# A two-layer hybrid encoder on one core: small operations moved between VectorE, ScalarE and GpSimd, maxima taken two key tiles later, one post step per key tile

## The chip, the cores and the metric

The kernel runs on 1 core of one Trainium2 chip. The metric is the device time of one execution in microseconds. The engines are called as in the profile: PE is TensorE (PEld its weight loads), DVE is VectorE, ACT is ScalarE, POOL is GpSimd, SP is SyncE, which issues nearly all DMAs.

## The reference

Two layers work on x of 2048 tokens by 1024 channels, in float32. What one layer computes, shortened:

```python
h = rmsnorm(x, pre_g[l])
u_a, v_a, g_a, q, k, v, g_b = split(h @ w_in[l])       # 512 512 512 512 128 128 512
y_a = gmlp_group(u_a, v_a, ...) * silu(g_a)            # layernorm of v_a, a 128x128 matrix
                                                       # per group over chunks of 128 tokens
y_b = gqa_axial_attention(q, k, v, ...) * silu(g_b)    # 8 query heads, 2 kv heads, head_dim 64
out = concat(y_a, y_b) @ w_out[l]
x = x + rmsnorm(out, post_g[l])
```

Queries and keys are normed per head and rotated (2-D axial rotary) before a full softmax attention over all 2048 keys.

## The kernel before

**Precision.** A float32 operand is split into a rounded "hi" and a residual "lo" (hi by ScalarE, lo by a subtraction on VectorE or GpSimd), and each product is the sum of hi·hi, hi·lo and lo·hi, the three `PASSES`.

**Projection stage (`Project.run`).** The 2048 tokens are four groups of 512, worked on in two halves of two groups. For a group, `hT_jobs` loads token tiles of 128 rows, norms them (two squares on ScalarE, a chain of small VectorE instructions `rsqrt_row_steps`, a multiplication by the gain row `g_row`), transposes them on TensorE and splits them into hi and lo. Blocks of 256 columns of w_in are loaded and split (`load_w`, `split_w`), and TensorE multiplies: keys and values (`do_kv`), queries (`do_q`), v_a (`do_va`), the attention gate (`do_gb`), the gMLP gate and u (`do_gate`). Small jobs are put off with `bg.add(delay, f)` and run by `bg.tick()`, which is called between the matmuls of a projection.

**g_row.** `norm_row` loads the norm gain, broadcast to 128 rows, and scales it by a constant (L185). For layer 0 it is called with the first token tile. For layer 1 it is asked for at key tile 1 of layer 0's attention, but as it is not pinned in order it is issued as soon as its buffer is free, which in the profile is inside layer 0's second projection half.

**Spatial weights.** `spatial_weights` transposes the gMLP matrices on TensorE into PSUM, copies them into `wsT` (L233), splits them and stores the parts to DRAM, from which they are loaded again as `ws`. Its four later jobs `b` compute a bias in PSUM and copy its two halves into `zbias` (L249, L250).

**Keys.** `k_t` holds hi and lo of the transposed keys. Rows 64 and 65 of the lo part hold ones (the memset at L1187), so that the second score matmul, whose query operand carries minus the maximum of each query row in two rows, subtracts that maximum while it adds the lo part.

**Attention stage (`attend`).** 32 units (4 query blocks of 512 by 8 heads) with 16 key tiles each make 512 key tiles in one loop over `k`. A key tile has two score matmuls into a bank `sp`, two exponentials by ScalarE (a float16 one, `p_hi`, and a float32 one, `p_f`), their difference `p_lo` (by GpSimd, for 15 of 100 key tiles by VectorE), and, some tiles later, the products with v and with ones (`po`, `sums`). Into this loop other work is woven:

- `later`, a table from key tile to jobs. For a later unit u, 16 steps `max_step` (a matmul into `pmax`, a VectorE maximum) are laid over `span` = 20 key tiles from `k0`; `max_row` follows at `k0 + span + 1`, `stack_max` at `k0 + span + 3`. The latter transposes the maxima on TensorE, makes two rows of them on ScalarE and VectorE, and stores them by two DMAs; `load_q` reads them back for the unit's scores.
- `fill`, a list of output steps: the product with w_out of an earlier query block, spread over the key tiles. A token tile's two halves are squared by ScalarE and multiplied by `g_post` on VectorE.
- `post_queue`: once a token tile's output is complete, `post_steps` appends the steps of its norm: eight small VectorE instructions, two residual adds of 128x512, the store, and, in layer 0 for the first eight token tiles, also layer 1's pre-norm (two squares, eight small steps, two scalings, a store to `h_d`), 24 steps in all. Up to two are taken in each key tile (L1107).

In the last query block the product with w_out is finished behind the attention (`last_steps`): there `post_steps` also multiplies by `g_post` in four pieces of 128x256 per token tile (`gain`, on GpSimd), and two token tiles' steps alternate.

**Order.** All instructions issued through `PE`, `ACT`, `DVE` and `POOL` keep their program order on their engine; this holds for all of the attention loop. Those through `nc.vector`, `nc.scalar`, `nc.gpsimd` and `nc.sync` are placed by a planner, which takes the earliest in program order among those that it holds to be ready, and may bring one far forward. Buffers come from rotating pools; token rows, `g_post`, `x_r` and `o_t` share five buffers "row", PSUM has seven banks "ps" beside `sums`.

Of the kernel before, what the change touches and what calls it, by code (L numbers as in the profile page):

```python
# [14 lines left out]
ALU = mybir.AluOpType  # L15
# [4 lines left out]
P = 128  # L20
# [5 lines left out]
HD = 64  # L26
# [8 lines left out]
NORM_SCALE = -8192.0 / D ** 0.5  # L35
# [3 lines left out]
def encoder(ctx: ExitStack, tc, x, w_in, w_out, pre_g, post_g, ln_a_g, ln_a_b,  # L39
# [135 lines left out]
    class Project:  # L175
# [5 lines left out]
        def norm_row(self):  # L181

            self.g_row = lay.tile([P, D], F32, name="g_row")
            nc.sync.dma_start(self.g_row, pre_g[self.l].partition_broadcast(P))
            nc.scalar.mul(self.g_row, self.g_row, 1.0 / NORM_SCALE)  # L185

        def begin(self):

# [26 lines left out]
        def spatial_weights(self):  # L215
            l = self.l
            self.lng = lay.tile([P, 4], F32, name="lng")
            nc.sync.dma_start(self.lng, ln_a_g[l].rearrange("(t p) -> p t", p=P))
            self.zbias = lay.tile([P, 4, P], F32, name="zbias")
            wsT = row_t("wsT")  # L220
            for hf in range(2):
                raw = f_t("fa")
                nc.sync.dma_start(raw.rearrange("p (g j) -> p g j", g=4),
                                  spatial_w[l, 4 * hf:4 * hf + 4].rearrange("g i j -> i g j"))
                hi = f_t("fh", dt=F32R)
                lo = f_t("fl", dt=F32R)

                def t(hf=hf, raw=raw, hi=hi, lo=lo):
                    ps = ps_t("pt")
                    for g in range(4):  # L230
                        PE.transpose(ps[:, g * P:(g + 1) * P], raw[:, g * P:(g + 1) * P], ident)
                    sl = slice(hf * GRP, (hf + 1) * GRP)
                    nc.vector.tensor_copy(wsT[:, sl], ps)  # L233
                    nc.scalar.copy(hi, wsT[:, sl])
                    nc.gpsimd.tensor_tensor(lo, wsT[:, sl], hi.bitcast(F32), ALU.subtract)
                    nc.sync.dma_start(ws_d[:, 0, sl], hi.bitcast(F32))
                    nc.sync.dma_start(ws_d[:, 1, sl], lo.bitcast(F32))
                bg.add(WS_DELAY + 2 * hf, t)
            lnb = f_t("fb")
            nc.sync.dma_start(lnb, ln_a_b[l].partition_broadcast(P))  # L240
            sb = row_t("sb_row", (1, D))
            nc.sync.dma_start(sb, spatial_b[l:l + 1].rearrange("o g i -> o (g i)"))
            for c in range(4):
                def b(c=c):
                    ps = ps_t("pt")
                    PE.matmul(ps[:, 0:2 * P], lnb[:, c * P:(c + 1) * P], wsT[:, 2 * c * P:(2 * c + 2) * P],
                              start=True, stop=False)
                    PE.matmul(ps[:, 0:2 * P], ones1, sb[:, 2 * c * P:(2 * c + 2) * P], start=False, stop=True)
                    nc.vector.tensor_copy(self.zbias[0:HD, c, :], ps[0:HD, 0:P])  # L249
                    nc.vector.tensor_copy(self.zbias[HD:P, c, :], ps[HD:P, P:2 * P])  # L250
                bg.add(WS_DELAY + 8 + 2 * c, b)

        def load_w(self, cols):
# [267 lines left out]
        def run(self, kv, first, last_jobs, first_wo):  # L521
# [5 lines left out]
            for n, gs in enumerate(halves):  # L527
                if len(gs) > 1:
                    hTs[gs[1]], preps, trans = self.hT_jobs(gs[1])
                    late = self.l == 0 and n == 0  # L530
                    for j, f in enumerate(preps):
                        if late:
                            bg.add(8 + j, f)
                        else:
                            f()
                    for m, f in enumerate(trans):
                        bg.add((13 if late else T_DELAY) + 3 * m // 2, f)
                if n == 0:
                    self.gains()
                w = self.split_w(self.load_w([C_Q]))  # L540
                for i, g in enumerate(gs):
                    if i == 0:
                        for f in self.stores:
                            f()
                        self.stores = []
                    if i == len(gs) - 1:
                        raw = self.load_w([C_Q + WB])
                    self.do_kv(g, self.banked(hTs[g], w_kv))
                    if i == len(gs) - 1:
                        w_next = self.split_w(raw)  # L550
                        raw = self.load_w([C_VA])
                    self.do_q(g, self.banked(hTs[g], w), 0)
                if n == 0:
                    self.spatial_weights()
                w = w_next
                for i, g in enumerate(gs):
                    self.do_q(g, self.banked(hTs[g], w), 1)
                    if i == 0:
                        w_next = self.split_w(raw)
                w = w_next  # L560
                raw = self.load_w([C_VA + WB])
                ws = [row_t("ws", dt=F32R) for _ in range(2)]
                for i in range(2):
                    nc.sync.dma_start(ws[i].bitcast(F32), ws_d[:, i])
                w = [w, self.split_w(raw)]
                raw = self.load_w([C_GB])
                for g in gs:
                    vs = []
                    for j in range(TPG):
                        ps = self.proj_tok(hTs[g], j, w[0])  # L570
                        self.proj_tok(hTs[g], j, w[1], ps, WB)
                        v = f_t("fv")
                        nc.scalar.copy(v, ps)
                        vs.append(v)
                    self.do_va(g, vs, ws)
                w = self.split_w(raw)
                blocks = [[C_GB + WB]] + [[C_GA + c * P, C_U + c * P] for c in range(4)]
                if n + 1 < len(halves):
                    blocks.append([C_K])
                if n + 1 == len(halves):  # L580
                    self.scale_v()
                    last_jobs()
                for b in range(2):
                    raw = self.load_w(blocks.pop(0))
                    for i, g in enumerate(gs):
                        self.do_gb(g, self.banked(hTs[g], w), b)
                        if i == 0:
                            w_next = self.split_w(raw)
                    w = w_next
                for c in range(4):  # L590
                    raw = self.load_w(blocks.pop(0)) if blocks else None
                    for i, g in enumerate(gs):
                        if i == len(gs) - 1 and c == 3 and n + 1 < len(halves):
                            g2 = halves[n + 1][0]
                            hTs[g2], preps, trans = self.hT_jobs(g2)
                            for j in range(TPG):
                                preps[j]()
                            for m, f in enumerate(trans):
                                bg.add(6 + 2 * m, f)
                        pg = self.proj_ch(hTs[g], w, 0)  # L600
                        pu = self.proj_ch(hTs[g], w, P)
                        self.do_gate(g, c, pg, pu)
                        if i == 0 and c == 3 and n + 1 == len(halves):
                            hTs[g] = None
                            first_wo()
                        if i == 0 and raw is not None:
                            w_next = self.split_w(raw)
                    w = w_next
                w_kv = w
                bg.flush()  # L610
# [18 lines left out]
    def attend(l, kv, nxt):  # L629
# [25 lines left out]
        def at(k, f):  # L655
            later.setdefault(k, []).append(f)
# [298 lines left out]
        def post_steps(s, t, last=False):  # L955
            z = small.tile([P, 1], F32, name="rs_o", bufs=4)

            def gain(i):
                sl = slice(i * WB, (i + 1) * WB)
                return lambda: POOL.tensor_tensor(s.o[:, sl], s.o[:, sl], g_post[:, sl], ALU.mult)  # L960

            def add(hf):
                def f():
# [80 lines left out]
        for u in range(pre, len(units)):  # L1044
# [3 lines left out]
            for n in range(steps):  # L1048
                at(k0 + n * span // steps, lambda u=u, n=n: max_step(u, n, PE, DVE))
            at(k0 + span + 1, lambda u=u: max_row(u, DVE))  # L1050
            at(k0 + span + 3, lambda u=u: stack_max(u, PE, ACT, DVE))

        def load_gb(u):
            qb, h = units[u]
# [37 lines left out]
        for k in range(end + 4):  # L1092
            if k < total:
# [10 lines left out]
                ACT.activation(p_f(k), sp, AF.Exp)  # L1104
                if not dve_share(k):
                    sub_lo(k, POOL)
            for _ in range(2):  # L1107
                if post_queue:
                    post_queue.pop(0)()
            kb = k - 1  # L1110
            if 0 <= kb < total and dve_share(kb):
                sub_lo(kb, DVE)
# [68 lines left out]
    for l in range(DEPTH):  # L1181
# [2 lines left out]
        v_t = big_t([P, 2, NT * NKV * HD], "v_st")  # L1184
        kv.append(v_t.bitcast(F32)[:, 0].rearrange("p (t k d) -> p t k d", t=NT, k=NKV))
        kv.append(v_t.bitcast(F16)[:, 1].rearrange("p (t k d) -> p t k d", t=NT, k=NKV))
        nc.vector.memset(kv[1][HD:HD + 2], 1.0)  # L1187
        att = attend(l, kv, layers[l + 1] if l + 1 < DEPTH else None)
        layers[l].run(kv, layers[l].first, *next(att))
        for _ in att:  # L1190
# [41 lines left out]
```

## Time and profile before

| | |
|---|---|
| time of three runs | 2773.86, 2774.44, 2772.46 us; median 2773.86 |
| the profiled execution's own time | 2771.47 us |
| its span (first to last instruction) | 2769.3 us |
| mean granted TensorE clock | 0.992 |
| busy: PE, DVE, ACT, POOL | 2677.1, 1896.8, 1522.7, 1287.0 us |

The times say how long an execution takes; the profile shows one execution. A timeline row gives start, duration, engine, line, operation, output<-input, shape and count, and in brackets how long the engine stood idle before it and what released it. A row of the waits gives who waited for whom, the total in us, how often, and the longest. A row by windows gives the window and its length, the busy time of PE, PEld, DVE, ACT and POOL with instruction counts, the granted clock, the DMA engines' share and GB/s. Line 84 is the helper through which every pinned instruction goes, so that these are told apart by the names of their tiles.

### The profile page before, as it was taken

Reading aid. Unit: us, or ns where it says so; the run is one execution under the profiler, and the core shown is the slowest. Engines: PE = TensorE matmul, PEld = TensorE weight load, DVE = VectorE, ACT = ScalarE, POOL = GpSimd, SP = SyncE. Lnnn points to the kernel's source line nnn. Section 1 sums busy time; section 2 is a strip of 40 time slices with the busy share of each in tenths; the row PEclk is TensorE's granted clock in tenths of the full one; section 3 lists DMA queues with packets and bytes.
Section 4 is the critical chain, followed back from the end, with each engine's and each line's share of the span. In section 5 each row is a group of like instructions: output and inputs, shape, how many; then the busy total and the mean of one; then the engine's idle time right before and its main releaser. Section 6 shows DMA issues by size and latency. Waiting matters only on the chain.

```text
span 2769.3 us, 48428 instructions
## 1 busy us (share of the span) xinstructions
PE 2677.1 (97%) x18230; PEld 1782.0 (64%) x18230; DVE 1896.8 (68%) x3796; ACT 1522.7 (55%) x3005; POOL 1287.0 (46%) x1080
## 2 busy tenths in 40 slices
PE   7999999999999999999999999999999999999997
PEld 6898899764444444444589989997644444444444
DVE  8862688876666776776487528888766666666664
ACT  4221432117887787787732214221288877778774
POOL 1210122007786676776632101210277767667765
PEclk9999999999999999999999999999999999999999
DMA  4424522322222232222354334333322222221313
GB/s 143 146 81 127 165 76 81 112 63 89 89 71 81 75 98 79 82 80 80 110 179 138 115 114 134 88 92 98 94 64 72 82 70 73 81 76 47 112 46 129
DMA packets 275310, 265.31 MB, mean 96 GB/s; under 512 B 19202, under 2 KB 233346, under 8 KB 275076
## 3 DMA queue, kind: packets, MB, share of 16 engines
q1 hardware_dynamic: 275076, 262.22, 30.2%
q8 instruction: 143, 2.34, 0.3%
q14 instruction: 91, 0.75, 0.1%
HBM read 177.09 MB, written 85.07 MB: 95 GB/s over the span
## 4 chain that ended last, share of the span: by engine, by line
PE 77%; DVE 11%; ACT 5%; DMA 3%; issue 2%; POOL 1%; SPq 0%; DVEq 0%; POOLq 0%; ACTq 0%
PE pp L84 27%; PE sp L84 14%; PE po L84 11%; PE pout L84 11%; PE pmax L84 7%; PE sums L84 4%; PE pt L84 2%; DVE fc L363 2%; ACT p_parts L84 2%; ACT p_f L84 2%; DMA w_raw<-in_w_in_dram 1%; DVE mx L84 1%; DVE o_t L84 1%; DVE w_lo L268 1%; ACT w_hi L267 1%
## 5 line engine op out<-in xcount | busy, mean ns | idle before, releaser
L84 POOL TENSOR_TENSOR p_parts<-p_f,p_parts 128x512 f16<-128x512 f32 x872 | 1034.9, 1205 | 404.2 <-ACT p_f L84 304.3
L84 ACT ACTIVATE p_parts<-sp 128x512 f16<-128x512 f32 x1024 | 630.0, 615 | 296.5 <-PE sp L84 289.8
L84 DVE TENSOR_REDUCE mx<-pmax 128x1 f32<-128x512 f32 x768 | 513.0, 681 | 211.9 <-PE pmax L84 209.9
L84 PE MATMUL pout<-wo,y_t 128*128 128x512 f32 x1488 | 657.1, 506 | 0.7 <-ACT p_f L84 0.3
L84 PE MATMUL po<-p_parts,v_st 128*32 128x512 f16 (+1 forms) x3072 | 639.2, 383 | 0.2
L84 ACT ACTIVATE p_f<-sp 128x512 f32<-128x512 f32 x1024 | 632.0, 617 | 0.0
L84 PE MATMUL pp<-w_hi,hT 128*128 128x256 f32 x3584 | 502.5, 290 | 16.1 <-DVE hT L310 9.7
L84 PEld LDWEIGHTS pp<-w_hi,hT 128*128 128x128 f32 x3584 | 462.0, 194 | 21.8 <-DVE hT L310 10.9
L84 PE MATMUL sp<-q_st,k_t 128*128 128x512 f16 x1024 | 390.2, 381 | 8.3 <-DVE mx L84 5.5
L84 PE MATMUL pmax<-k_t,q_m 128*128 128x512 f16 x1024 | 389.7, 382 | 7.6 <-DVE mx L84 3.2
L84 PEld LDWEIGHTS <-v_st 128*32 128x32 f16 (+1 forms) x3072 | 193.7, 96 | 309.5 <-issue 253.0
L84 PE MATMUL sp<-q,k_t 66*128 66x512 f16 x1024 | 391.0, 382 | 0.0
L84 PEld LDWEIGHTS pout<-wo,y_t 128*128 128x128 f32 x1488 | 281.3, 190 | 128.4 <-issue 8.7
L84 PEld LDWEIGHTS <-k_t 128*128 128x128 f16 (+1 forms) x2048 | 191.5, 99 | 187.7 <-issue 74.4
L468 POOL TENSOR_TENSOR fl<-fa,fh 128x512 fp32r<-128x512 f32 x32 | 43.1, 1346 | 533.3 <-ACT fh L467 489.2
L84 PE MATMUL pp<-hT,w_hi 128*128 128x512 f32 x1024 | 271.7, 413 | 0.0
L84 PE MATMUL pp<-w_lo,hT 128*128 128x256 f32 x1792 | 262.6, 290 | 0.0
L84 PE MATMUL sums<-p_parts,one_h 128*32 128x512 f16 x2048 | 242.3, 380 | 0.0
L84 PEld LDWEIGHTS pp<-w_lo,hT 128*128 128x128 f32 x1792 | 235.5, 194 | 0.9
L84 PEld LDWEIGHTS pp<-hT,w_hi 128*128 128x128 f32 x1024 | 193.4, 190 | 35.3
L683 DVE TENSOR_REDUCE mx<-pmax 128x1 f32<-128x512 f32 x256 | 172.6, 687 | 49.1 <-PE pmax L84 47.5
L84 PEld LDWEIGHTS <-q_m 128*128 128x128 f16 x1024 | 99.8, 98 | 140.2 <-issue 42.1
(161 smaller groups left out, 2790.9 us busy)
## 6 DMA issues: line engine op xcount, KB each, us to landing
w_raw<-in_w_in_dram SPq DMA_DIRECT2D x28, 1024.0 KB
y_t<-y_d SPq DMA_DIRECT2D x56, 512.0 KB
w_raw<-in_w_in_dram SPq DMA_DIRECT2D x32, 512.0 KB
x_t<-in_x_dram SPq DMA_DIRECT2D x16, 512.0 KB
z_d<-fb SPq DMA_DIRECT2D x32, 256.0 KB
gb_d<-fa SPq DMA_DIRECT2D x32, 256.0 KB
fb<-z_d SPq DMA_DIRECT2D x32, 256.0 KB
y_d<-fh SPq DMA_DIRECT2D x32, 256.0 KB
```

The source lines that it names most:

```text
L84: return tc.keep_in_program_order(call(*args, **kw))
L267: nc.scalar.copy(hi[:, sl], raw[:, sl])
L268: nc.vector.tensor_tensor(lo[:, sl], raw[:, sl], hi.bitcast(F32)[:, sl], ALU.subtract)
L363: nc.vector.tensor_tensor(t2[:, :, :, lo:lo + 16], qn[:, :, :, hi:hi + 16], tbi[:, :, 1:2, lo:lo + 16].broadcast_to([P, 2, n, 16]), ALU.mult)
L468: nc.gpsimd.tensor_tensor(lo, th, hi.bitcast(F32), ALU.subtract)
L683: dve.tensor_reduce(s.mx[:, j, c:c + 1], ps, AX.X, ALU.max)
```

## The change

Seven edits:

1. `g_row` is scaled by GpSimd instead of ScalarE, in both layers.
2. `wsT` is copied out of PSUM by ScalarE instead of VectorE.
3. So is `zbias`.
4. The rows of ones in the keys are filled by GpSimd, and in program order not ahead of the layer but in its second projection half, before `scale_v`.
5. `stack_max` comes two key tiles later.
6. One post step is taken in each key tile instead of up to two.
7. In the last layer the last token tile's four multiplications by `g_post` are done by VectorE.

```diff
             nc.sync.dma_start(self.g_row, pre_g[self.l].partition_broadcast(P))
-            nc.scalar.mul(self.g_row, self.g_row, 1.0 / NORM_SCALE)
+            nc.gpsimd.tensor_scalar(self.g_row, self.g_row, 1.0 / NORM_SCALE, None, ALU.mult)
...
-                    nc.vector.tensor_copy(wsT[:, sl], ps)
+                    nc.scalar.copy(wsT[:, sl], ps)
...
-                    nc.vector.tensor_copy(self.zbias[0:HD, c, :], ps[0:HD, 0:P])
-                    nc.vector.tensor_copy(self.zbias[HD:P, c, :], ps[HD:P, P:2 * P])
+                    nc.scalar.copy(self.zbias[0:HD, c, :], ps[0:HD, 0:P])
+                    nc.scalar.copy(self.zbias[HD:P, c, :], ps[HD:P, P:2 * P])
...
                 if n + 1 == len(halves):
+                    nc.gpsimd.memset(self.kv[1][HD:HD + 2], 1.0)
                     self.scale_v()
...
-                return lambda: POOL.tensor_tensor(s.o[:, sl], s.o[:, sl], g_post[:, sl], ALU.mult)
+                engine = DVE if nxt is None and t == NT - 1 else POOL
+                return lambda: engine.tensor_tensor(s.o[:, sl], s.o[:, sl], g_post[:, sl], ALU.mult)
...
-            at(k0 + span + 3, lambda u=u: stack_max(u, PE, ACT, DVE))
+            at(k0 + span + 5, lambda u=u: stack_max(u, PE, ACT, DVE))
...
-            for _ in range(2):
-                if post_queue:
-                    post_queue.pop(0)()
+            if post_queue:
+                post_queue.pop(0)()
...
-        nc.vector.memset(kv[1][HD:HD + 2], 1.0)
```

## The prediction

> **What bounds the kernel now.** I read the page first, then the windows by stage, then TensorE's waits, then the timeline at each long wait.
>
> ```profile
> span 2769.3 us, 48428 instructions
> ...
> PE 2677.1 (97%) x18230; PEld 1782.0 (64%) x18230; DVE 1896.8 (68%) x3796; ACT 1522.7 (55%) x3005; POOL 1287.0 (46%) x1080
> ```
> ```profile
> 620.00:1366.00 746.00, 729.21 (x4963) 345.25 (x4962) 494.93 (x878) 589.17 (x1186) 536.40 (x448) 1.00 0.26 82
> 1990.00:2724.00 734.00, 722.45 (x4952) 342.69 (x4950) 463.03 (x797) 578.26 (x1150) 529.95 (x447) 1.00 0.24 78
> ```
>
> TensorE is busy for 2677.1 of 2769.3 us, so 92.2 us of its idle time are all there is to win, beside time at a low granted clock. The window rows (length, then PE, weight loads, DVE, ACT, POOL, clock) put 16.8 and 11.5 us of that into the two attention stages. The rest lies at the start, in the projections, at the layer switch and behind the last matmul. So each edit is priced by the TensorE wait that it touches, not by the engine time that it moves.
>
> **The change part by part.** *Start of layer 0 (g_row scaled by POOL, memset off DVE).*
>
> ```profile
> 0.73 0.20 POOL masks.py:197 MEMSET ident<- 128x128 f32 x1 [0.29 <-POOLq L1219]
> ...
> 6.67 1.06 ACT L185 ACTIVATE g_row<-g_row 128x1024 f32<-128x1024 f32 x1 [1.57 <-DMA g_row<-in_pre_g_dram]
> ...
> 7.64 0.58 ACT L294 ACTIVATE sq<-x_t 128x512 f32<-128x512 f32 x1
> ...
> 12.71 1.94 PE L84 MATMUL pt<-ident,x_t 128*128 128x128 f32 x8 [12.71 <-DVE x_t L299]
> ...
> 21.93 3.47 DVE L1187 MEMSET k_t<- 2x4096 f16 x1 [0.91 <-issue]
> ...
> 28.57 0.68 DVE L310 TENSOR_TENSOR hT<-pt,hT 128x512 fp32r<-128x512 f32 x1
> ...
> 29.31 1.23 PE L84 MATMUL pp<-w_hi,hT 128*128 128x256 f32 x4 [4.57 <-DVE hT L310]
> ...
> 32.28 1.05 ACT L267 CAST w_hi<-w_raw 128x1024 fp32r<-128x1024 f32 x1 [6.03 <-DMA w_raw<-in_w_in_dram]
> ```
>
> ACT stood from 6.67-1.57=5.10 to 7.64 before its second square, 2.54 us, on which the first transpose (12.71) hangs through DVE's chain. On POOL the scaling costs between ACT's 1.06 us and four two-input passes of 12.10/15=0.81 us (row of the last stage, below), 3.2 us; I take 1.6, near the lower end since it reads one tensor. It is then ready by 8.3 us, ahead of that chain. Gain 2.5 us. Without the memset DVE reaches the subtraction of 28.57 up to 3.47 us sooner and the 4.57 us wait shrinks by that. Together 6.0; but the next weights arrive only at 32.28, their cast waits 6.03 us for the DMA, and they become the next thing late: I take 5, ends 2 and 8.5 (with clock, below). On POOL the memset costs between 0.20 us (its small memset) and 0.20x32=6.4 us by element count; I take DVE's 3.5. POOL's next rows are the cover: it can run any time after the tile is free, ahead of work that idles anyway (15.65 us idle, below). If that cover is gone, 3.5 us fall on a rope product or a residual split. Its reader, the second score matmul, comes only in the attention stage.
>
> *Layer switch.*
>
> ```profile
> 1400.88 3.47 DVE L1187 MEMSET k_t<- 2x4096 f16 x1 [0.91 <-issue]
> 1404.38 4.88 DVE L84 TENSOR_TENSOR hT<-pt,hT 128x512 fp32r<-128x512 f32 x8
> ...
> 1405.13 1.12 PE L84 MATMUL pt<-ident,x_h 128*128 128x128 f32 x4 [4.49 <-DVE hT L84]
> ```
> ```profile
> 28.00:36.00 8.00, 6.44 (x35) 6.15 (x35) 7.86 (x19) 3.72 (x7) 1.27 (x1) 0.60 0.45 129
> 1405.00:1410.00 5.00, 4.87 (x23) 4.87 (x24) 5.00 (x13) 0.59 (x1) 2.42 (x3) 0.51 0.16 52
> ```
>
> Here the memset stands alone in front of the subtractions that TensorE waits for: 3.47 us go straight off. After both 4.5 us waits the granted clock falls, to 0.60 and 0.51; at 0.51, 4.87 busy us hold 0.49x4.87=2.4 us of loss. A wait of 1.0 us should not bring this: gain 5.5, ends 3.4 and 5.9. [...]
>
> *g_row of layer 1, loaded inside layer 0.*
>
> ```profile
> 336.91 1.06 ACT L185 ACTIVATE g_row<-g_row 128x1024 f32<-128x1024 f32 x1 [6.23 <-DMA g_row<-in_pre_g_dram]
> ...
> 338.54 0.42 DVE L351 TENSOR_REDUCE ms_q<-fb 128x4 f32<-128x256 f32 x1 [4.53 <-ACT fb L350]
> ...
> 342.79 0.77 POOL L360 TENSOR_TENSOR fc<-fc,fa 128x256 f32<-128x256 f32 x1 [15.65 <-DVE fc L358]
> ...
> 392.27 0.67 PE L84 MATMUL pt<-ident,fc 128*128 128x128 f32 x4 [3.00 <-DVE fc L365]
> ```
>
> ACT, in order, stands 6.23 us for this DMA, with squares and casts queued behind it; DVE idles 4.53 us for one of them, and TensorE pays later, 3.00 us at 392. The wait moves to POOL, which idles 15.65 us there; the rope product behind it comes perhaps 1 us late. Gain 3.5, ends 0 and 6.
>
> *wsT and zbias on ACT.*
>
> ```profile
> 123.23 2.05 PE L84 MATMUL pp<-w_hi,hT 128*128 128x256 f32 x8 [2.47 <-DVE zbias L250]
> ...
> 127.12 0.59 ACT L573 COPY fv<-pp 128x512 f32<-128x512 f32 x1 [5.73 <-DVE fc L365]
> ...
> 1497.08 1.19 PE L84 MATMUL pp<-w_hi,hT 128*128 128x256 f32 x8 [2.04 <-DVE zbias L250]
> ...
> 1752.63 0.37 ACT L395 CAST k_t<-pt 128x256 f16<-128x256 f32 x1 [3.24 <-PE pt L84]
> ```
>
> TensorE waits 2.47 and 2.04 us for zbias copies late on a full DVE. On ACT each costs at most the 0.37 us of a larger PSUM copy, 8 per layer, and 2 wsT copies, in slack: ACT idled 5.73 us at that place. But that idle is a blocked fv copy: a zbias copy queued behind it would end at 127.7, 4.5 us later than now. Ends: loss of 2x4.5=9, gain of 4.5 plus the slow 2.05-1.19=0.86. I take 3, since the zbias job is emitted before fv in program order.
>
> *Attention: later maxima, one post step.*
>
> ```profile
> PE sp L84 <- DVE mx L84: 5.2, 5, 1.9
> PE t L84 <- DVE m_neg L84: 3.1, 4, 1.1
> ```
> ```profile
> PE t L84 <- DVE m_neg L84: 3.3, 5, 1.1
> PE pmax L84 <- DVE mx L84: 2.9, 2, 1.5
> ```
> ```profile
> 951.51 3.03 DVE L84 SCALAR_TENSOR_TENSOR o_t<-o_t,rs_o,x_r 128x512 f32<-128x512 f32 x2
> ```
> ```profile
> 955.20 0.38 PE L84 MATMUL sp<-q_st,k_t 128*128 128x512 f16 x1 [1.90 <-DVE mx L84]
> ```
>
> The waits are of layer 0, then layer 1. The transpose of the maxima waits 6.4 us in all, never above 1.1; two key tiles more (746/512=1.5 us each) cover that. Its ACT copy, DVE subtraction and two SP stores move too; the last unit's read needs them 10 key tiles on. Gain 4.5, ends 0 and 6.4. Two residual adds in one key tile hold DVE 3.03 us, and the score bank behind them comes 1.90 us late; one per tile halves the burst, and 24 steps then reach over 24 key tiles instead of 12. Where the last stage empties the queue, about 7 steps are left instead of 3, on a DVE that has no maxima left to reduce: nothing. Of 5.2+2.9=8.1 us I take 5; ends 8 and -3 (new coincidences).
>
> *Tail.*
>
> ```profile
> 2741.39 0.42 DVE L84 TENSOR_TENSOR gb<-gb,rden 128x256 f32<-128x256 f32 x1
> ...
> 2751.56 12.10 POOL L84 TENSOR_TENSOR o_t<-o_t,g_post 128x256 f32<-128x256 f32 x15 [0.62 <-ACT pout L84]
> ...
> 2756.28 4.75 DVE L84 SCALAR_TENSOR_TENSOR o_t<-o_t,rs_o,x_w 128x512 f32<-128x512 f32 x4
> ...
> 2760.96 0.32 DVE L84 TENSOR_SCALAR rs_m<-ss_o 128x1 f32<-128x1 f32 x2
> ...
> 2763.28 2.92 DVE L84 SCALAR_TENSOR_TENSOR o_t<-o_t,rs_o,x_w 128x512 f32<-128x512 f32 x4
> ```
>
> Here the edit costs. POOL ends at 2763.66, 0.4 us after DVE is ready for the last adds: the two are level. Tile 15's four gains enter DVE's order behind the adds that end at 2761.03, and nothing hides them: 4x0.42=1.7, less the 0.4. Loss 1.5, ends 0 and 3. [...]
>
> **The sum.** 5+5.5+3.5+3+4.5+5-1.5=25.0 us off the profiled execution's 2771.5 (span 2769.3 plus 2.2 around it): 2746.5. The three runs' median is 2773.9, 2.4 above, so 2749 us there. 0.2% is 5.5 us, about what a measurement of this kernel tells from no change.
>
> **Rivals.** (a) The zbias copies queue behind fv: 3 gained become 9 lost; 2761. For it: the 5.73 us row. (b) TensorE's attention waits only change names (a copy or an exp ends next): 9.5 lost from the sum; 2758. For it: DVE is as full as before. (c) Start and projections give nothing, because weights and rope DMAs are next: only attention less tail, 8.0; 2766. For it: the 6.03 us row. (b) and (c) together: no change, 2774. (d) Slower: the post steps of a tile no longer end before the row buffers are asked for again.
>
> ```profile
> 903.85 0.69 DVE L84 TENSOR_TENSOR o_t<-pout,g_post 128x512 f32<-128x512 f32 x1 [0.79 <-ACT o_t L84]
> ...
> 943.92 0.69 DVE L84 TENSOR_TENSOR o_t<-pout,g_post 128x512 f32<-128x512 f32 x1 [1.02 <-ACT o_t L84]
> ```
> ```profile
> 923.07 0.32 SPq L992 DMA_DIRECT2D h_d<-x_r  x1
> 923.49 0.39 SPq L834 DMA_DIRECT2D x_r<-in_x_dram  x1
> ```
>
> Tiles' outputs come 40.07 us apart; 24 steps at two took 923.07-903.85=19.2 us, at one 38.4, so the store falls at 942.3, 1.6 us ahead of the next output, and the load of x_r behind it on SP as late. It decides if the freed rows come after the next ACT square into o_t, half a tile (20 us) on: ACT would stop the exponentials. At 5 us for each of 6 tiles: 30 lost, 2779. Against it: those 20 us.
>
> **How the numbers follow.** Forecast 0.48 (2741 to 2756), (a) 0.13, (b) 0.15, (c) 0.10, (b) with (c) 0.07, (d) 0.07. Faster by over 0.2%: 0.48+0.13+0.15 and 0.08 of (c), 0.84; within: 0.02+0.07=0.09; slower 0.07. The range runs from 2739 (a further 10 of the upper ends) to 2767, past (c).
>
> **What would show it.** Right: first transpose near 10 us; no wait above 2 us at 29 and at the switch, clock there near 1.0; TensorE's wait for m_neg near zero; POOL idle, not ACT, ahead of g_row; the tail from the last matmul to the end longer by 1 to 3 us. Wrong: zbias waits that name ACT, p_parts or m_rows in place of mx, or a memset before a residual split on POOL.

## The result, and the profile after

The changed kernel takes 2749.36 us (median of four runs, 2748.69 to 2749.49), the kernel before 2773.16 us beside it (2770.90 to 2774.44): a ratio of 0.9915, 95% interval 0.9897 to 0.9932. 23.8 us are gone; 25.0 were predicted, which put the median at 2749. The total came out as said; several of its terms did not.

The head of the page of the changed kernel and, of its windows, the two attention stages and the places of three long waits, at the start, at the switch and for zbias (columns as before):

```profile
span 2747.6 us, 48433 instructions
...
PE 2670.1 (97%) x18230; PEld 1778.0 (65%) x18230; DVE 1853.6 (67%) x3778; ACT 1524.5 (55%) x3023; POOL 1296.4 (47%) x1080
...
611.00:1357.00 746.00, 732.19 (x4982) 348.33 (x4981) 483.67 (x891) 590.22 (x1192) 538.00 (x449) 1.00 0.26 83
1969.00:2703.00 734.00, 725.50 (x4966) 345.18 (x4965) 454.11 (x804) 578.56 (x1153) 530.22 (x449) 1.00 0.25 79
27.00:35.00 8.00, 4.56 (x27) 4.56 (x28) 5.43 (x13) 2.37 (x8) 4.57 (x2) 0.79 0.62 189
1389.00:1394.00 5.00, 4.71 (x30) 4.52 (x30) 5.00 (x11) 3.12 (x7) 5.00 (x9) 0.70 0.91 294
118.00:128.00 10.00, 10.00 (x78) 9.17 (x77) 6.20 (x12) 2.38 (x7) 4.35 (x3) 1.00 0.92 302
```

TensorE was idle for 92.2 us of its span and is now for 77.5. The granted clock is 1.00 at 118 to 128 us, where the wait for zbias was; at the start and the switch it is still 0.79 and 0.70, against 0.60 and 0.51 before. TensorE's busy time fell too, from 2677.1 to 2670.1 us for the same 18230 matmuls: up to the last pd (a small product with `den`, the last mark but one below) the clock was at half speed for nine stretches of 3.41 us before and for five after, and such a stretch costs up to 1.7 us, an estimate: half of 3.41, where TensorE is busy throughout. So of the 21.7 us by which the span is shorter 14.7 are idle time and 7.0 are clock.

TensorE runs the same work in both kernels, so the place of a fixed instruction gives each stage's length. The marks are the starts of eight TensorE rows, and the end of the span: the projection that waits for k_t at 103.10 (after: 102.09), the transpose of ws of layer 0 that waits for fl at 183.29 (177.16), the maximum's matmul that waits for fb at 498.63 (490.75), the last pd of layer 0 at 1383.18 (1371.06), the first transposes of kk of layer 1 at 1441.92 (1425.25), the transpose of ws that waits for fl at 1555.66 (1536.70), the maximum's matmul that waits for fb at 1865.81 (1846.06), the last pd at 2740.87 (2717.90), the end at 2769.3 (2747.6). The table gives how much longer (+) or shorter (-) than before each stage is, in us, in one profile of each kernel; the experiments follow below.

| stage, by marks of before | predicted | all edits | ones' fill on GpSimd | g_row | zbias and wsT | one post step | later maxima |
|---|---|---|---|---|---|---|---|
| 0 to 103, start | -5 | -1.01 | -2.29 | +0.40 | +0.78 | +0.55 | +0.99 |
| to 183, zbias | -1.5 | -5.12 | -1.76 | -1.47 | -5.12 | +1.26 | -0.12 |
| to 499, second half | -3.5 | -1.75 | +0.76 | -2.63 | +1.04 | +0.69 | +0.71 |
| to 1383, attention 0 | -9.5 with attention 1 | -4.24 | -0.09 | -1.39 | -0.67 | -2.57 | -1.77 |
| to 1442, switch | -5.5 | -4.55 | -5.95 | +0.36 | -0.17 | -0.50 | +0.55 |
| to 1556, zbias | -1.5 | -2.29 | +1.78 | +3.83 | -2.29 | +2.20 | +0.33 |
| to 1866, second half | 0 | -0.79 | -0.91 | +1.76 | +0.60 | -1.04 | -0.87 |
| to 2741, attention 1 | above | -3.22 | +0.04 | -0.03 | +0.30 | -2.02 | -0.36 |
| to the end, tail | +1.5 | +1.27 | -0.18 | +0.07 | -0.17 | +1.13 | +0.04 |

The column of all edits adds up to the spans' 21.70 us. Entries of 0.5 to 2.2 us in stages that an edit doesn't touch are the scatter of the start and of the granted clock (last section), and an entry is to be read with that: the -1.76 and -1.47 to 183 stand for a low clock that did not follow the wait for zbias in those two profiles, the +2.20 and +3.83 to 1556 for one that did follow there; the 1.13 us of one post step in the tail lies behind the last adds, in the last store. Of the 3 us predicted for zbias and wsT each layer's stage is given half.

### The profile page after: what moved, and what is told of

It reads as the page before. It is cut to its first block, busy times and chain, and to the rows that moved or that the text cites. A ratio compares the mean times of both kernels' runs of the same rounds, so it can differ in the third digit from the quotient of the medians.

```text
span 2747.6 us, 48433 instructions
## 1 busy us (share of the span) xinstructions
PE 2670.1 (97%) x18230; PEld 1778.0 (65%) x18230; DVE 1853.6 (67%) x3778; ACT 1524.5 (55%) x3023; POOL 1296.4 (47%) x1080
## 4 chain that ended last, share of the span: by engine, by line
PE 82%; DVE 8%; ACT 5%; DMA 2%; issue 1%; POOL 1%; SPq 0%; DVEq 0%; POOLq 0%; ACTq 0%
PE pp L84 30%; PE sp L84 14%; PE pout L84 12%; PE po L84 12%; PE pmax L84 7%; PE sums L84 4%; PE pt L84 3%; ACT p_parts L84 2%; ACT p_f L84 1%; DVE fc L363 1%; DMA w_raw<-in_w_in_dram 1%; DVE mx L84 1%; DVE w_lo L268 1%; DVE p_parts L84 1%; DVE o_t L84 1%
```

## The experiments

Where a kernel's time is given, its kernel before ran beside it, at 2773.0 to 2773.7 us.

**1. The ones' fill alone.** The kernel before with edit 4.

> Edit 4 alone (rows of ones by GpSimd, late in program order). Theory A: it pays only where the memset stands directly ahead of the subtractions that TensorE waits for, at the layer switch: the 4.49 us wait shrinks to about 1 and the low clock behind it goes, 4 to 6 us faster in all, and nothing at the start of layer 0, where the wait near 29 us stays above 4 us because the next weights' cast sits behind a DMA. Rival B (the prediction): the wait near 29 us shrinks by 3 us as well, 7 to 9 us faster in all. Rival C: the planner only rearranges, within 2 us.

2764.97 us (2762.82 to 2771.08), ratio 0.9972 [0.9958, 0.9985]. 8.4 us by the medians, which is theory B's 7 to 9: the stage table has 2.3 us at the start and 5.95 at the switch. TensorE's rows at the switch, in its timeline:

```profile
1396.51 0.66 PE L84 MATMUL pt<-ident,x_h 128*128 128x128 f32 x4 [1.57 <-ACT pout L84]
1397.71 0.66 PE L84 MATMUL pt<-ident,x_h 128*128 128x128 f32 x4 [0.54 <-DVE hT L84]
```

The wait for hT is 0.54 us instead of 4.49, and the four transposes behind it take 0.66 us, where before they took 1.12 at the low clock. But 1.78 us of this are lost again before 1556: TensorE comes sooner to zbias, still on VectorE, and waits 2.40 us for it instead of 2.04, 0.66 for wsT, which it had not waited for, and 0.23 for k_t.

**2. g_row on GpSimd alone.** The kernel before with edit 1.

> Edit 1 alone (g_row scaled by GpSimd). Theory A: first transpose near 10.4 us instead of 12.7, first projection matmul at 15.3 to 15.5 as before, because ScalarE casts weights and squares three more half rows ahead of it; the gain is that of layer 0's second half alone, 2 to 4 us. Rival B (the prediction): 2.5 us at the start and 3.5 us in the second half, 6 us. Rival C: no gain, since GpSimd's wait for the row holds up the rope product.

2769.06 us, ratio 0.9984 [0.9974, 0.9993], 4.3 us by the medians. At the start nothing is gained (+0.40), as theory A has it; 2.6 us come off layer 0's second half. In layer 1 the edit touches nothing, and the 3.83 us there are a low clock (0.71 at 1490 to 1500) that this one execution had and that before did not.

**3. zbias and wsT on ScalarE, then zbias alone.** The kernel before with edits 2 and 3; and with edit 3.

> Edits 2 and 3 alone (wsT and zbias copied by ScalarE). Theory A: both waits for zbias (2.47 and 2.04 us) and the low clock behind the first one go, and with them the small waits for wsT and k_t: 5 us in layer 0 and 2 us in layer 1, 6 to 8 us in all. Rival B (the prediction): 3 us. Rival C: the zbias copies queue behind the blocked fv copy, 9 us slower.

> The kernel before with edit 3 alone (zbias copied by ScalarE, wsT still by VectorE). Theory A (zbias is nearly all of the gain of edits 2 and 3, which took 5.1 us between TensorE times 103 and 183 us): the wait of 0.66 us for wsT at 112 us stays, the one of 2.47 us for zbias goes, the stage loses 4 to 4.5 us, and no wait names a ScalarE copy. Theory B (VectorE was late through both): with wsT on it another wait takes the place, and the stage loses under 3 us. Theory C (zbias behind the blocked fv copy): the stage becomes up to 4 us longer.

Both: 2763.72 us, ratio 0.9963 [0.9948, 0.9978]. zbias alone: 2765.23 us, ratio 0.9974 [0.9963, 0.9984]. In zbias alone's profile the two stages lose 4.19 and 1.21 us, with both edits 5.12 and 2.29; the 0.67 us wait for wsT stays, that for zbias is gone and the clock at its place is whole. TensorE's timeline and a window of zbias alone, then of before:

```profile
112.59 0.70 PE L84 MATMUL pt<-wsT,fb 128*128 128x256 f32 x2 [0.67 <-DVE wsT L233]
...
119.00:129.00 10.00, 10.00 (x73) 8.67 (x73) 9.00 (x25) 3.02 (x8) 4.34 (x3) 1.00 0.90 289
```

```profile
118.00:128.00 10.00, 7.53 (x39) 6.00 (x38) 9.48 (x25) 1.76 (x3) 4.08 (x3) 0.83 0.92 288
```

So zbias carries the edit, wsT has about 1 us in each layer. The low clock is in the profile of before, but not in every one: in those of experiments 1 and 2 the same wait, 2.18 and 2.48 us, brought none, so that some 1.5 us of the 5.12 are not always there to win. Rival (a) falls by its price and not by its mechanism: in the changed kernel ScalarE does six of layer 0's eight copies between other work, but the last two do stand behind an fv copy that was blocked for 6.25 us, and end 4.7 and 4.9 us after their matmul did. No wait of TensorE names them. The first of the eight, the fv copy and the seventh:

```profile
113.35 0.25 ACT L249 COPY zbias<-pt 64x128 f32<-64x128 f32 x1
...
125.70 0.59 ACT L573 COPY fv<-pp 128x512 f32<-128x512 f32 x1 [6.25 <-DVE fc L365]
126.18 0.26 ACT L249 COPY zbias<-pt 64x128 f32<-64x128 f32 x1
```

**4. One post step alone; later maxima alone; all but later maxima.** The kernel before with edit 6; with edit 5; the changed kernel without edit 5.

```diff
-            for _ in range(2):
-                if post_queue:
-                    post_queue.pop(0)()
+            if post_queue:
+                post_queue.pop(0)()
```

> Edit 6 alone (one post step per key tile). Theory A: the waits of the scores for mx behind two adds in one key tile (1.90 and 1.91 us in layer 0, 1.47 and 1.48 in layer 1) go, one of about 2 us is new: 4 to 6 us in all. Rival B: nothing, the burst is only moved, within 2 us. Rival C: the row buffers come free too late, slower than before.

> The kernel before with edit 5 alone (the maxima's transposes two key tiles later). Theory A (VectorE's backlog is the limit there, and the wait for m_neg is only its first name): the 6.4 us of waits for m_neg vanish, waits of 0.3 to 0.8 us of pmax for mx appear in the key tiles behind, and the two attention stages together lose 3 to 4 us; both stages of the changed kernel lost 7.5 us and one post step alone lost 4.0 us of them. Theory B (the wait is freed in full): 6 to 6.5 us, no new waits. Theory C (only names change): under 1 us.

> The changed kernel without edit 5 (maxima's transposes at their old place). Theory A (the two attention edits add, with little shared): TensorE's waits for m_neg come back and the two attention stages become 2.1 to 2.9 us longer, as edit 5 alone took 2.1 us off and both together 7.5, one post step alone 4.6; 2751.5 to 2752.3 us. Theory B (one post step a key tile already removes VectorE's lateness for m_neg): under 1 us longer.

One post step: 2769.49 us, ratio 0.9983 [0.9973, 0.9993], 4.6 us in the attention stages. Later maxima: 2770.19 us, ratio 0.9991 [0.9983, 1.0], an interval that reaches no change; 2.1 us there by the profile: less than the 3 to 4 of theory A, far from B's 6, and above C's 1. In both profiles the attention stages hold as much time at a low clock as before, so that the comparison is one of waits. Without edit 5: 2751.93 us (2751.12 to 2752.99), all four runs above all four of the changed kernel; its stages lose 3.61 and 2.30 us instead of 4.24 and 3.22. So edit 5 is worth 1.6 us there by the stages, which is between the two theories, and edit 6 the larger part. The medians differ by 2.6 us, as theory A has it, but the profile without edit 5 is also 1.5 us later at the start, which that edit doesn't touch.

TensorE's waits in attention 0 (who waits for whom: us in total, times, longest), of later maxima alone, of one post step alone, and of both in the changed kernel, which answer to the rows of layer 0 before (sp for mx 5.2, t for m_neg 3.1):

```profile
PE sp L84 <- DVE mx L84: 4.5, 4, 1.9
PE pmax L84 <- DVE mx L84: 2.1, 4, 0.8
PE sp L84 <- ACT p_f L84: 1.8, 3, 1.3
...
PE pmax L84 <- DVE m_rows L84: 0.8, 1, 0.8
```
```profile
PE t L84 <- DVE m_neg L84: 5.0, 6, 1.3
PE pmax L84 <- DVE mx L84: 2.5, 2, 2.2
PE pmax L84 <- DVE o_pair L84: 1.5, 2, 0.8
```
```profile
PE pmax L84 <- DVE mx L84: 4.8, 6, 2.3
PE sp L84 <- ACT p_f L84: 2.0, 3, 1.4
PE pmax L84 <- DVE o_pair L84: 1.5, 2, 0.9
```

Later maxima: the waits for m_neg are gone, and 2.1 us of pmax for mx, 1.3 more of sp for p_f and 0.8 for m_rows stand in their place. One post step: of the 5.2 us of sp for mx 0.3 are left; 2.5 us of pmax for mx, one wait of 2.2 us among them, are new, as theory A has it, and m_neg comes later still, 5.0 instead of 3.1. VectorE shows why, in the changed kernel ahead of a wait of 0.81 us (TensorE's row is the last):

```profile
755.21 0.69 DVE L84 TENSOR_TENSOR o_pair<-po,o_pair 64x512 f32<-64x512 f32 x1 [1.53 <-ACT o_pair L84]
755.93 0.72 DVE L84 STREAM_TRANSPOSE den<-sums 128x512 f32<-128x512 f32 x1
756.68 1.39 DVE L84 TENSOR_TENSOR p_parts<-p_f,p_parts 128x512 f16<-128x512 f32 x1
758.00 0.68 DVE L84 TENSOR_REDUCE mx<-pmax 128x1 f32<-128x512 f32 x1
758.60 0.15 DVE L84 TENSOR_REDUCE m_neg<-mx 128x4 f32<-128x16 f32 x1
...
758.72 0.38 PE L84 MATMUL pmax<-k_t,q_m 128*128 128x512 f16 x1 [0.81 <-DVE mx L84]
```

Here, and in the same way ahead of the waits of 0.81 us at 2113.2 and 2341.0, it has the pair's sum, the denominators' transpose and a p_parts in one row, each instruction started as the last one ends, and mx, which TensorE needs for the next bank of PSUM, stands behind them, whether or not the transposes of m_neg are asked for at that moment.

**5. The last tile's gains back on GpSimd.** The changed kernel without edit 7.

> The changed kernel without edit 7 (the last tile's four multiplications by g_post back on GpSimd). Theory A (VectorE's order sets the end): 1.3 us faster than the changed kernel, some 2748 us; from the last matmul group behind the denominators (pd) to the end 28.4 us instead of 29.7. Theory B (GpSimd's fifteen multiplications or the last store set the end as well): the tail stays at 29.7 us, time as the changed kernel.

The tail is 28.44 us instead of 29.70 (theory A). By time, 2748.68 us (2748.10 to 2749.93), ratio 0.9914 [0.9900, 0.9927]: 0.7 us below the changed kernel, which is not to be told apart in four runs. VectorE's rows of the tail, changed kernel first:

```profile
2733.33 4.76 DVE L84 SCALAR_TENSOR_TENSOR o_t<-o_t,rs_o,x_w 128x512 f32<-128x512 f32 x4
2738.02 1.42 DVE L84 TENSOR_TENSOR o_t<-o_t,g_post 128x256 f32<-128x256 f32 x4
...
2741.67 2.74 DVE L84 SCALAR_TENSOR_TENSOR o_t<-o_t,rs_o,x_w 128x512 f32<-128x512 f32 x4
```
```profile
2733.97 4.76 DVE L84 SCALAR_TENSOR_TENSOR o_t<-o_t,rs_o,x_w 128x512 f32<-128x512 f32 x4
...
2740.96 2.92 DVE L84 SCALAR_TENSOR_TENSOR o_t<-o_t,rs_o,x_w 128x512 f32<-128x512 f32 x4
```

From the first adds to the last: 8.34 us with the gains on VectorE, 6.99 without.

**6. The start: g_row of layer 0 back on ScalarE; an earlier cast.** The changed kernel with each.

```diff
+            if self.l == 0: nc.scalar.mul(self.g_row, self.g_row, 1.0 / NORM_SCALE)
+            else: nc.gpsimd.tensor_scalar(self.g_row, ...)
```
```diff
-        if j == 2:
+        if j == 0:
             for f in trans[:2]:
```

> The changed kernel with g_row of layer 0 scaled by ScalarE as before, and that of layer 1 by GpSimd. Theory A (moving layer 0's scaling brings the first transposes forward by 2.3 us but nothing that follows, and costs at the second wait, since g_row alone left TensorE 0.4 us later at 103 us and the memset alone 2.3 us earlier): first transposes at 12.7 us, and the matmul that the changed kernel has at 102.1 us comes 0.5 to 1.3 us sooner. Theory B (the scaling on GpSimd helps the start): it comes 1 to 2.5 us later than 102.1 us. Nothing else moves by more than the clock's chance at waits of 2.1 us.

> The changed kernel, in whose start of layer 0 the first two jobs that transpose and split a token group are emitted two tiles earlier in program order, so that ScalarE's first cast of hT no longer stands behind the squares of later tiles. Theory A (ScalarE's order ate the 2.3 us by which the first transposes came sooner, and the next weights set the following wait): first products at 12.5 to 13.5 us instead of 15.5, the wait near 30 us longer by as much, and the matmul at 102.1 us moves by less than 1 us. Theory B (the lead is carried on): it comes 2 to 2.5 us sooner. Theory C (the squares put back become the next thing late): it comes 1 to 2 us later.

The first: 2746.41 us, ratio 0.9905 [0.9891, 0.9918]; its four runs (2745.80 to 2746.71) all lie below the changed kernel's, and the mark at 102.09 comes at 101.20, as theory A has it. Only 0.9 of the 3.1 us between the two spans lie there; 2.4 are in the second half and at the switch, where this profile had one stretch of low clock less in each. The second: 2747.65 us, ratio 0.9910 [0.9893, 0.9926]; first products at 12.68 us instead of 15.49, the mark at 100.72. That is 1.4 us sooner, more than theory A's 1 and less than B's 2 to 2.5: part of the lead is carried on, if one profile can say so.

One execution's start scatters by 1 to 1.5 us, so the mark is better read over all profiles: 103.10 to 104.09 in the five with the start of before (or only wsT changed), 102.09 to 103.58 in the three with g_row on GpSimd and the fill moved, 100.81 to 102.18 in the three with the fill moved alone. By the means (103.66, 102.90, 101.40) moving g_row costs 1.5 us of the 2.3 that the fill gives. Alone, without the fill moved, it costs nothing (103.50). The rows of the changed kernel (TensorE, GpSimd, ScalarE, VectorE), then with g_row on ScalarE (TensorE, VectorE):

```profile
10.41 1.97 PE L84 MATMUL pt<-ident,x_t 128*128 128x128 f32 x8 [10.41 <-DVE x_t L299]
15.49 2.32 PE L84 MATMUL pp<-w_hi,hT 128*128 128x256 f32 x8 [3.11 <-ACT hT L309]
...
30.44 2.93 PE L84 MATMUL pp<-w_hi,hT 128*128 128x256 f32 x12 [5.56 <-DVE hT L310]
...
6.80 2.77 POOL L185 TENSOR_SCALAR g_row<-g_row 128x1024 f32<-128x1024 f32 x1 [5.50 <-DMA g_row<-in_pre_g_dram]
...
10.04 2.18 ACT L267 CAST w_hi<-w_raw 128x512 fp32r<-128x512 f32 x4 [4.22 <-DMA w_raw<-in_w_in_dram]
...
14.87 0.57 ACT L309 CAST hT<-pt 128x512 fp32r<-128x512 f32 x1
...
28.38 1.41 DVE L299 SCALAR_TENSOR_TENSOR x_t<-x_t,rs_x,g_row 128x512 f32<-128x512 f32 x2
29.70 1.88 DVE L310 TENSOR_TENSOR hT<-pt,hT 128x512 fp32r<-128x512 f32 x3
```
```profile
28.57 2.93 PE L84 MATMUL pp<-w_hi,hT 128*128 128x256 f32 x12 [3.38 <-DVE hT L313]
...
27.83 0.68 DVE L313 TENSOR_TENSOR hT<-pt,hT 128x512 fp32r<-128x512 f32 x1
```

The first transposes do come 2.3 us sooner. Then ScalarE does four weight casts and four squares of later tiles before it casts hT at 14.87, exactly when it did with the later transposes, and the first products stay at 15.49; in the second of these kernels, with that cast at 12.05, they come at 12.68. And the planner's order on VectorE shifts with it: from 27.6 us, after the same weights, it takes two scalings of x_t before hT at 29.70, where it had taken hT at 27.83.

**7. Put together.** g_row of layer 0 on ScalarE with the last gains on GpSimd; and the earlier cast on top.

> The changed kernel with g_row of layer 0 on ScalarE and the last tile's multiplications by g_post on GpSimd. Theory A (the two effects are apart in time and add): 1.3 us below the 2746.4 us of the kernel with the first alone, 2745.1 us; tail 28.4 us. Theory B (they don't add): 2746.4 us or more.

> The kernel before this one in the list (g_row of layer 0 on ScalarE, last multiplications on GpSimd) with the earlier emission of the first two transposing jobs as well. Theory A (with the first transposes at 12.7 us the first weights, not ScalarE's order, are what the first products wait for): within 1 us of that kernel everywhere. Theory B (ScalarE's order matters here too): first products up to 1 us before 15.5 us, and the matmul at 101.2 us as much sooner.

The first: 2746.69 us (2744.42 to 2747.68), ratio 0.9903 [0.9889, 0.9918], not the 2745.1 of theory A, though its tail is 28.4 us; its start was at the late end (102.18) and it had a low clock at 310 us that the kernel of experiment 6 was spared. The second: 2744.17 us (2740.51 to 2747.33), ratio 0.9895 [0.9880, 0.9910], first products at 14.59 us, 0.9 us sooner as theory B has it, the mark at 100.57; but as this profile had no stretch of low clock at the start and the other had two, the mark does not decide between the theories. It is the lowest median, but its interval takes in the others': that it is the best is not shown.

## Why the prediction came out, point by point

**Start: the step that failed (5 predicted, 1.0 measured).** The price of g_row on GpSimd was 2.77 us, not the 1.6 taken, inside the bounds; so it was not ready ahead of VectorE's chain, as said, and VectorE stood 0.97 us for it. That alone was harmless: the transposes came at 10.41 as predicted. What failed is "Gain 2.5 us" for them: their reader, the cast of hT, stood in ScalarE's order behind other work and did not move. The fill's share was right as a mechanism (waits of 3.0 to 3.8 us at 28 us in the three profiles with the fill moved and g_row on ScalarE, 4.3 to 5.4 us at 29 us in the five with the start of before), and 2.3 us in size. "No wait above 2 us at 29" and "clock there near 1.0" did not come true: 5.56 us and 0.79. The bounds 2 to 8.5 didn't hold the 1.0, and even that is clock: the changed kernel's profile has one stretch of low clock at the start where before has two. Two other profiles with the same start have two, and there the start is 0.08 us shorter and 0.48 us longer than before.

**Switch: right.** 5.5 predicted; 5.4 to 6.0 us in six of the eight profiles with the fill moved, 4.55 in the changed kernel's own and 4.12 in one other, where two waits brought a low clock after all. TensorE's rows in the changed kernel:

```profile
1388.28 0.91 PE L84 MATMUL pt<-ident,x_h 128*128 128x128 f32 x4 [1.79 <-ACT pout L84]
1389.48 1.12 PE L84 MATMUL pt<-ident,x_h 128*128 128x128 f32 x4 [0.29 <-DVE hT L84]
```

The wait for pout, hidden in part before (1.07), is what is late next.

**g_row of layer 1: the wait moved as said, what it had cost was misplaced, 3.5 against 1.75.** 2.6 us in its own run, 2.8 with g_row of layer 1 alone on GpSimd. In the changed kernel's profile 1.75, as a low clock followed the wait at 313 us. "POOL idle, not ACT" came true, though the first row names a VectorE instruction as the last releaser and not the DMA:

```profile
332.17 2.78 POOL L185 TENSOR_SCALAR g_row<-g_row 128x1024 f32<-128x1024 f32 x1 [12.04 <-DVE fc L358]
...
379.86 1.28 POOL L342 TENSOR_TENSOR fa<-fa,gain_q 128x512 f32<-128x512 f32 x1 [11.36 <-DMA fa<-in_rope_dram]
...
384.42 0.66 PE L84 MATMUL pt<-ident,fc 128*128 128x128 f32 x4 [2.02 <-DVE fc L365]
```

But "TensorE pays later, 3.00 us at 392" was the wrong place. That wait is still there in the changed kernel, 2.02 us at 384.42, and 2.2 to 2.6 us in six of the seven others with this edit (in the last it is split in two); a rope product on GpSimd, which stands 11.36 us for its own DMA there and stood 10.70 before, comes late just ahead of it. What the edit took away are three short waits right behind the scaling, 0.35, 0.63 and 0.49 us at 339.8 to 342.8 in the profile of before.

**zbias and wsT: under-sized, 3 against 7.4.** The upper bound named for the waits was 5.4 us (2.47, 2.04 and the slow 0.86), and 3 was taken between it and rival (a). The reason given against that rival, that the zbias job is emitted before fv, did not hold for the last two copies of layer 0; that they cost nothing was not foreseen. The rest was not in the sum: the low clock behind the wait cost more than the one row quoted (0.83 over 118 to 128 us, 1.7 us at most against the 0.86), and the wait of 0.66 us for wsT went as well. Some 0.5 us are left, in waits too short to be told apart.

**Attention: over-sized, 9.5 against 7.5.** One post step was nearly exact (5 predicted, 4.6 alone). The later maxima were taken at 4.5 and are 2.1 alone: rival (b) is right for the larger part of this edit, and wrong for the other. "TensorE's wait for m_neg near zero" came true and meant little, since the lateness is VectorE's and not the transpose's. The sum counted waits, and the waits above 0.2 us of both stages fell by 5.4 us only, from 26.3 to 20.9; most of the rest is a low clock that followed two waits of 1.9 us in layer 0 before and one of 2.28 after. In the two profiles in which that one brought no low clock, both with the attention stages of the changed kernel, these lose 9.4 and 9.7 us.

**Tail: right.** 1.5 predicted, 1.27 measured; experiment 5 takes it off again. GpSimd ending level with VectorE was read correctly. In the changed kernel VectorE's first four adds, up to 2738.1, took 1.19 us each (4.76/4), most of them beside GpSimd's last multiplications, which ended at 2737.55, and its last four 0.69 (2.74/4); its four gains began after that end, at 2738.02.

**Fill's cost: right.** 3.50 us, taken at VectorE's 3.5, and no row of the profile waits for it.

The total agrees because the start's 4.0, g_row's 1.75, the switch's 0.95 and the attention's 2.0 us too much were met by 4.4 us too little for zbias, 0.8 by the clock in a stage that no edit touches, and 0.2 in the tail: 21.7 by the spans against 25.0. The medians, 23.8 apart, are kinder to it, since the profiled execution of before was 1.7 us below its median. It is a right total, by luck, on terms of which three are wrong by 2 to 4.4 us; and 7.0 of the 21.7 us are clock, of which the sum had priced only the stretches at the start, at the switch and, in part, behind zbias. The edits made singly take 8.4, 4.3, 9.6, 3.8 and 2.8 us off by their medians, less the tail's 1.3: 27.6, more than the 23.8 of all together by 3.8, of which the start may explain 1.5; the rest is within the intervals of the ratios.

## What to carry to other kernels

Look up what stands ahead of the reader of an operation that becomes ready sooner: here the first transposes came 2.3 us sooner, and as the cast that reads them stood behind other work on ScalarE until 14.87 us, the first products stayed at 15.49. Where a wait names a small instruction at the end of a burst, move the burst's parts apart rather than the instruction: here the first took 4.6 us off the attention stages, the second 2.1. Price a wait at a place with a low clock by a window over that place, and take several profiles before a term of 2 us is called measured: here the same wait of 2.13 us was followed by 3.41 us at half speed in twelve of 28 cases, up to 1.7 us more, and by full speed in the others, as told next.

## What the hardware showed that was not expected

**The same wait was followed by a low clock in some cases and not in others.** In each of the fourteen profiles TensorE waits 2.13 us for hT near 313 and near 1680 us. In twelve of these 28 the clock then was at half speed for 3.41 us (0.83 over 10 us), in sixteen at full speed. The changed kernel has one of each (timeline and windows):

```profile
313.20 1.98 PE L84 MATMUL pp<-w_hi,hT 128*128 128x256 f32 x8 [2.13 <-DVE hT L310]
...
1672.73 1.22 PE L84 MATMUL pp<-w_hi,hT 128*128 128x256 f32 x8 [2.13 <-DVE hT L310]
...
309.94:313.35 3.41, 1.28 (x12) 1.04 (x11) 3.41 (x6) 3.41 (x9) 0.19 (x1) 1.00 0.83 286
313.35:316.76 3.41, 3.41 (x17) 3.41 (x18) 3.41 (x14) 3.38 (x13) 1.09 (x1) 0.50 0.91 306
1668.44:1671.86 3.42, 2.17 (x20) 1.93 (x18) 3.40 (x5) 3.18 (x8) 0.00 (x0) 1.00 0.56 169
1671.86:1675.27 3.41, 2.54 (x21) 2.54 (x22) 3.41 (x9) 3.41 (x12) 1.30 (x1) 1.00 0.97 287
1675.27:1678.68 3.41, 3.41 (x31) 3.41 (x30) 3.41 (x18) 1.79 (x6) 0.00 (x0) 1.00 1.00 320
```

The windows are cells of a grid that the traces' clock records show. In every profile all changes of the granted clock, 160 in the fourteen, 15 of them in that of before and 11 in that of the changed kernel, lie on multiples of 3.4133 us from one another, to within 0.002 us; where the grid begins differs from profile to profile. The wait at 313.20 lies in one cell, which has TensorE busy for 1.28 of its 3.41 us, and the next cell is at half speed. The wait at 1672.73 is cut in two by a border of the grid, each cell is busy for over 2 us, and the clock stays. In the profile of before the waits end at 319.32 and 1691.69; the first has 1.64 us in one cell and full speed behind it, the second 1.85 and half speed. This sorts all 28: the twelve waits with 1.85 us or more in one cell were followed by the low clock, the sixteen with at most 1.77 us in one cell were not. Over all cells at full clock between 40 and 2700 us, 10850 of them, each of the 50 in which TensorE idled for more than 1.82 us was followed by half speed, and of the others three; in the profiles of before and of the changed kernel alone it is nine of nine, and one of the others, with 1.79 us.

So what looks like chance goes, in these profiles, with the place of a wait in that grid, and the grid begins elsewhere in each of them. Up to the last pd the fourteen profiles have between two and ten cells at half speed, nine before and five after, at up to 1.7 us each. The wait of 4.49 us at the switch, longer than a cell, was followed by it in all six profiles that have it, the 1.6 to 1.8 us in its place in two of eight. The scatter of the times goes with it: of 45 executions of the kernel before, the nine with a mean clock of 0.991 or less took 2774.9 to 2779.1 us, the sixteen with 0.993 or more 2769.0 to 2773.1.

**GpSimd's price was VectorE's for one operation and 2.6 times ScalarE's for another.** The fill takes 3.50 us on it (timeline of the changed kernel) and 3.47 on VectorE, but the scaling of 128x1024 float32 by a constant 2.77 against ScalarE's 1.06.

```profile
31.72 3.50 POOL L581 MEMSET k_t<- 2x4096 f16 x1
```

The scaling reads one tensor; it took 2.77 us in layer 0 and 2.78 in layer 1, against the 1.06 of ScalarE in each. No run here scales that row on VectorE.
